# A transformer layer on one core: the modulation stage in another order, and half of the gate-weight rounds moved to a later stage

## The chip, the cores and the metric

The kernel runs on 1 of the 8 cores of a Trainium2 chip. The metric is the device time of one execution in microseconds (us). The engines are named as the profile names them: PE is TensorE (matrix multiplication), DVE is VectorE, ACT is ScalarE, POOL is GpSimd, SP is SyncE, which here issues all the DMAs from one queue. All data are 32-bit; the matrix products are made from a high and a low part of each operand, three products for one, so that they keep the accuracy of 32 bits.

## The reference

One layer of a generator works on 1024 latent tokens (rows of x) and 256 context tokens, each 1024 wide. Cut to what matters here:

```
mod = silu(c) @ w_ada + b_ada          # 6 sections of 1024: shift, scale, gate, shift, scale, gate
mod_c = silu(c_ctx) @ w_ada + b_ada    # the same for the context tokens
px = (rms_norm(x, g_pre_mix) * (1 + scale) + shift) @ w_in      # and pc from ctx, with mod_c
# the columns of px: attention q, k, v; mLSTM q, k, v, output gate, and 16 gate values a token
att = window_attention(...)            # 8 heads, band of 128, all context keys, a sink
h   = mlstm(...)                       # 4 heads, forward and backward, with a state from the context
x   = x + gate * rms_norm(concat(att, h) @ w_out)
x   = x + gate_f * rms_norm(swiglu(modulated norm of x))
```

Only the first part concerns the change: the shift and scale of the first sub-layer, the modulated tokens, their product with w_in, and the gate weights of the mLSTM, which for each chunk of 128 tokens n and each direction d are exp(a + u + mask), a 128 x 128 matrix for each of 4 heads.

## The kernel before

The tokens lie in 10 tiles of 128: tiles 0 to 7 are latent, 8 and 9 are context. Work goes through stages.

*The modulation stage.* Shift and scale come in quarters q = 0 to 3, each 256 columns of both sections. A quarter needs four weight tiles wm (512 KB each). pr_mm(q, h) is half h of its product on TensorE (8 matmuls), mod_row(q) takes the result out of PSUM with ScalarE and VectorE, mod_t(q) turns it into columns (4 transposes), and mod_col(q) adds up and multiplies on VectorE, into hs. In the meantime tiles 0, 1 and 2 (ET = 3) are normalised: prep_c(i) squares on ScalarE, takes the root there and the reciprocal on VectorE, and scales the tile on GpSimd; its two parts can be called apart. prep_t(i) transposes the tile on TensorE, and t_cp(i, b, engine) copies half b out of PSUM. For a quarter q of a tile i, h_ts (VectorE) applies scale and shift, h_hi (ScalarE) makes the high part hh, h_lo (VectorE) the low part hl. w_hi and w_lo do the same for that quarter of the weight columns (w1 is 272 wide, w2 is 384). sq(i, q) then does the 12 matmuls of tile i and quarter q into two PSUM tiles ("slab"); a callback can be put in its middle. warm(n) issues n matmuls of ones that nothing reads. ld("...") gives the order of the loads: x is a token tile, m a wm tile, w a quarter of the weight columns. The order of all this is written out by hand: pin keeps an instruction behind what was traced before it on its engine.

*The slab stage.* Tiles 3 to 9 go through prep_l (load), prep_c, prep_t, prep_m, prep_b and then s1 (24 matmuls with the 272 columns) and s2 (24 with the 384). For tiles 6 to 9 a transposed copy (xtr) is loaded as hraw, and only the root is spread over partitions by a matmul (L235); eight VectorE steps (L256) scale it. gates() works out the gate values in a long chain of small operations, with s2 of tiles 4 to 9 as TensorE's other work.

*Gate weights.* ml_weights(n), for n = 0 to 7, loads two rows of a_d, spread over 128 partitions (256 KB each), does 8 VectorE additions (L640) and 2 exponentials on ScalarE (L641) on them, and stores 512 KB in w_dr[n] (L642). Eight such rounds stand here. The attention stage loads w_dr[n] back (ml_load, L897).

*The transposed stage.* For the 13 tiles of 128 columns in TILES (mk0, mk1, ak, mq0, mq1, aq0 to aq3, mo0 to mo3), tload(j) loads and splits the weights, tproj multiplies, and a convolution, a rotation or a sigmoid follows. From mq0 on, state_step (transposes pk at L803, key scratch at L805, products pu at L809) advances the mLSTM state after each tile, in 9 steps. ada_rest sums up the later modulation sections on VectorE (L751) from loads of 512 KB.

*The attention and mLSTM stage* has 16 items of half a block; the first eight also do one mLSTM block each (ml_scores, ml_values at L1053 and L1057). What follows, the output projection and the feed-forward part, is not touched.

The scratch buffers R0 to R15 are 16 regions of SBUF. R(k, name, shape) gives region k to a new tile. A new tile in a region waits for the last use of the one before it, wherever in the program that use is written. So mkc, the context keys with the scratch kps of all state steps, keeps region 8 until the last state step. Region 8 is also that of the round weights w2 and w7, and of qz of the second mLSTM block.

Outside the pinned instructions a planner orders each engine's work by a timing model of its own.

## Time and profile before

| | us |
|---|---|
| median of 3 runs (lowest, highest) | 1179.77 (1179.26, 1180.34) |
| the profiled execution's own time | 1177.58 |
| its span in the trace | 1175.8 |

| engine | busy us | share of the span |
|---|---|---|
| PE | 1153.5 | 98% |
| DVE | 774.1 | 66% |
| ACT | 551.0 | 47% |
| POOL | 147.5 | 13% |

The span is the time from the first to the last instruction in the trace, 1.8 us less than the execution's own time. Matmuls overlap, so a busy PE is not necessarily at its peak. The mean granted clock of TensorE is 0.997. Rows of the trace begin with the start and the length in us, then engine, source line, operation, output and inputs; "x8" is the number of instructions in the row, and in brackets stands how long the engine had been idle and what ended it.

### The profile page before, as it was taken

What the parts mean: (1) busy time and instruction counts of PE and PEld (TensorE: products, weight loads), DVE (VectorE), ACT (ScalarE), POOL (GpSimd) and SP (SyncE); (2) the same over time, 40 slices, a digit from 0 to 9 for tenths busy, and PEclk for the clock granted to TensorE, in tenths of its full rate; (3) what the DMA queues carried; (4) which work ended last, traced back from release to release, by engine and by line L of the source; (5) the groups of instructions that cost most, each with busy time, mean ns of one, the idle gap of its engine ahead of it and who ended that gap; (6) DMA issues with size and microseconds to landing.
All of it is one profiled execution on the core that took longest, in us unless ns stands there. A gap on an engine that the chain in (4) does not pass through costs nothing.

```text
span 1175.8 us, 16321 instructions
## 1 busy us (share of the span) xinstructions
PE 1153.5 (98%) x5905; PEld 950.8 (81%) x5905; DVE 774.1 (66%) x1417; ACT 551.0 (47%) x1032; POOL 147.5 (13%) x200
## 2 busy tenths in 40 slices
PE   8989989999999999999999999999999999999997
PEld 6789878878888777888788888888888888888886
DVE  4673858882787653469677767777677756644557
ACT  4553444222777864887443333333343434434543
POOL 1240002144655640000000000000000000000000
PEclk9999999999999999999999999999999999999999
DMA  9621954657798605220334566555644458666853
GB/s 372 228 95 50 382 218 133 196 168 220 224 247 217 179 19 179 92 88 36 99 135 159 196 219 223 206 206 213 220 158 140 174 200 271 208 207 193 298 189 125
DMA packets 102984, 216.99 MB, mean 185 GB/s; under 512 B 10228, under 2 KB 39540, under 8 KB 101496
## 3 DMA queue, kind: packets, MB, share of 16 engines
q1 hardware_dynamic: 102904, 215.95, 55.3%
q8 instruction: 46, 0.75, 0.3%
q14 instruction: 34, 0.28, 0.1%
HBM read 159.29 MB, written 55.97 MB: 183 GB/s over the span
## 4 chain that ended last, share of the span: by engine, by line
PE 94%; DVE 3%; ACT 1%; DMA 1%; issue 0%; DVEq 0%; SPq 0%; POOL 0%; ACTq 0%; POOLq 0%
PE xv L79 8%; PE xv L77 8%; PE xv L78 8%; PE pt L79 6%; PE pt L77 6%; PE pt L78 6%; PE t L701 4%; PE t L700 4%; PE t L703 4%; PE pt L1155 3%; PE pt L1137 3%; PE op L79 2%; PE op L78 2%; PE op L77 2%; PE fx L77 2%; PE fx L79 2%
## 5 line engine op out<-in xcount | busy, mean ns | idle before, releaser
L66 DVE TENSOR_TENSOR fo<-fr,fo 128x1024 fp32r<-128x1024 f32 x77 | 93.0, 1223 | 72.4 <-ACT fo L65 69.3
L65 ACT CAST fo<-fr 128x1024 fp32r<-128x1024 f32 x77 | 79.5, 1051 | 74.0 <-PE pt L79 34.8
L700 PE MATMUL t<-hh,th 128*128 128x512 f32 x208 | 82.6, 398 | 0.0
L701 PE MATMUL t<-hl,th 128*128 128x512 f32 x208 | 81.9, 394 | 0.0
L1537 ACT CAST wS<-wr 128x512 fp32r<-128x512 f32 x88 | 54.2, 622 | 55.4 <-PE pt L79 36.8
L1539 DVE TENSOR_TENSOR wS<-wr,wS 128x512 fp32r<-128x512 f32 x88 | 60.4, 689 | 19.8 <-ACT wS L1537 19.7
L703 PE MATMUL t<-hh,tl 128*128 128x512 f32 x208 | 66.6, 394 | 0.0
L79 PE MATMUL xv<-tT,wS 128*128 128x512 f32 x168 | 65.7, 391 | 0.0
L77 PE MATMUL xv<-tT,wS 128*128 128x512 f32 x168 | 65.7, 391 | 0.0
L78 PE MATMUL xv<-tT,wS 128*128 128x512 f32 x168 | 65.6, 390 | 0.0
L77 PE MATMUL op<-woh,mh 128*128 128x512 f32 x128 | 50.9, 398 | 0.0
L79 PE MATMUL op<-woh,ml 128*128 128x512 f32 x128 | 50.1, 392 | 0.6 <-DVE ml L66 0.6
L78 PE MATMUL op<-wol,mh 128*128 128x512 f32 x128 | 50.0, 391 | 0.0
L1285 DVE TENSOR_TENSOR wr<-wr 128x512 f32<-128x512 f32 x66 | 45.5, 690 | 1.4
L700 PEld LDWEIGHTS t<-hh,th 128*128 128x128 f32 x208 | 39.4, 189 | 8.4 <-issue 0.3
L701 PEld LDWEIGHTS t<-hl,th 128*128 128x128 f32 x208 | 39.4, 189 | 7.8 <-issue 0.8
L1571 ACT ACTIVATE es<-es 128x512 f32<-128x512 f32 x22 | 13.9, 632 | 66.5 <-DVE es L1288 66.5
L703 PEld LDWEIGHTS t<-hh,tl 128*128 128x128 f32 x208 | 37.8, 189 | 7.0 <-issue 0.5
L77 PE MATMUL pt<-fo 128*128 128x512 f32 x110 | 42.8, 389 | 0.0
L78 PE MATMUL pt<-fo 128*128 128x512 f32 x110 | 42.8, 389 | 0.0
L79 PE MATMUL pt<-fo 128*128 128x512 f32 x110 | 42.8, 389 | 0.0
L874 PE MATMUL s<-k,qh 128*128 128x256 f32 (+1 forms) x128 | 41.7, 336 | 0.5 <-DVE sm L876 0.5
(792 smaller groups left out, 3303.2 us busy)
## 6 DMA issues: line engine op xcount, KB each, us to landing
wr<-in_wfi SPq DMA_DIRECT2D x44, 512.0 KB, 5.0
wb<-in_wada SPq DMA_DIRECT2D x24, 512.0 KB, 7.6
s_d<-a SPq DMA_DIRECT2D x22, 512.0 KB, 6.4
bt<-in_wfo SPq DMA_DIRECT2D x44, 256.0 KB, 3.7
tb_d<-bt SPq DMA_DIRECT2D x11, 1024.0 KB, 3.8
fr<-s_d SPq DMA_DIRECT2D x44, 256.0 KB, 4.3
fr<-tb_d SPq DMA_DIRECT2D x44, 256.0 KB, 4.3
fr<-a_d SPq DMA_DIRECT2D x33, 256.0 KB, 4.5
```

Of the source, the lines that this page charges most:

```text
L65: act.copy(hi, raw)
L66: dve.tensor_tensor(lo, raw, hi.bitcast(F32), SUB)
L77: pe.matmul(ps, a[0], b[0], start=first, stop=False, **kw)
L78: pe.matmul(ps, a[0], b[1], start=False, stop=False, **kw)
L79: pe.matmul(ps, a[1], b[0], start=False, stop=last, **kw)
L700: pe.matmul(o, wh[:, kt], m[0], start=f, stop=False)
L701: pe.matmul(o, wh[:, kt], m[1], start=False, stop=False)
L703: pe.matmul(o, wl[:, kt], m[0], start=False, stop=l)
L874: pe.matmul(o, qh[:, h, :], k2[g][:, kc], start=True, stop=False)
L1285: dve.tensor_tensor(out, a, b, SUB)
L1537: act.copy(w[:, 0], raw)
L1539: dve.tensor_tensor(w[:, 1], raw, w[:, 0].bitcast(F32), SUB)
```

## The change

- The ten token tiles and their scratch hraw get other regions (the two lists of region numbers in prep_l); x1 and x2 are loaded earlier, and all remaining tile loads are queued before the loop over the slabs.
- The stage's order is rewritten: tile 1 and tile 2 are prepared earlier, the high halves of the weight columns are made one by one, and tile 1's transposes go into the middle of the first sq. In sq the products with the low half of the tokens come last. The fillers warm(1) and warm(3) go, warm(6) becomes warm(8). Two more PSUM tiles use the tag tp. The evictions of tiles 0 to 2 are pinned, and tile 5's normalisation comes behind the first of them.
- ml_weights(0) to (3) stay where they are, in regions 6, 7, 8 and 15. Rounds 4 to 7 are written at the ends of the tiles mo0, mo1 and mo2 of the transposed stage, all in region 8.

```diff
@@ -197,19 +197,19 @@
     def prep_l(i):
 
         j = i - NT
-        xt = xts[i] = R(4 + i % 4, f"xt{i}", (D,))
+        xt = xts[i] = R((4, 5, 6, 7, 4, 5, 10, 6, 13, 15)[i], f"xt{i}", (D,))
         xd[i] = dma(xt, x[i * P:(i + 1) * P] if i < NT else ctx[j * P:(j + 1) * P])
-        hraw[i] = R((0, 1, 2, 3, 10, 11, 12, 13, 8, 9)[i], f"hraw{i}", (KT, P))
+        hraw[i] = R((0, 1, 2, 3, 8, 9, 11, 12, 14, 7)[i], f"hraw{i}", (KT, P))
         return xd[i]
 
     def prep_c(i, parts=(0, 1)):
 
         xt, r = xts[i], st[:, 10 + i:11 + i]
-        if 1 not in parts:
+        if parts == (0,):
             pin(act.activation(hraw[i].rearrange("p a b -> p (a b)"), xt, AF.Square, accum_out=st[:, i:i + 1]))
             pin(act.activation(r, st[:, i:i + 1], AF.Sqrt, bias=epst, scale=1.0 / D))
             return
-        if 0 not in parts:
+        if parts == (1,):
             pin(dve.reciprocal(r, r))
             pin(pool.tensor_scalar(xt, xt, r, 1.0, MUL, MUL))
             return
@@ -299,7 +299,7 @@
 
     def pr_mm(q, h):
         if not h:
-            prs_[q] = pa.tile([P, 512], F32, name=f"pr{q}", tag="gx" if q < 3 else "tp", bufs=2)
+            prs_[q] = pa.tile([P, 512], F32, name=f"pr{q}", tag="gx" if q < 2 else "tp", bufs=2)
         for t in range(4):
             pin(pe.matmul(prs_[q][32 * t:32 * t + 32], cz[:, 4 * h + t, :], was[q, 2 * h + t // 2][:, t % 2],
                           start=not h, stop=h == 1))
@@ -311,7 +311,7 @@
     pcl = {}
 
     def mod_t(q):
-        pcl[q] = pa.tile([P, 4, P], F32, name=f"pcol{q}", tag="gx" if q < 2 else "tp", bufs=2)
+        pcl[q] = pa.tile([P, 4, P], F32, name=f"pcol{q}", tag="gx" if q < 1 else "tp", bufs=2)
         for k in range(4):
             pin(pe.transpose(pcl[q][:, k, :], rr[:, k * P:(k + 1) * P], ident))
 
@@ -332,9 +332,9 @@
         return ((w1h[b][:, k:k + 2], w1l[b][:, k:k + 2], w[:, 0:544].rearrange("p (k n) -> p k n", k=2)),
                 (w2h[b][:, k:k + 2], w2l[b][:, k:k + 2], w[:, 544:1312].rearrange("p (k n) -> p k n", k=2)))
 
-    def w_hi(q):
-        for h_, l_, w in w_(q):
-            pin(act.copy(h_, w))
+    def w_hi(q, i):
+        h_, l_, w = w_(q)[i]
+        pin(act.copy(h_, w))
 
     def w_lo(q, i):
         h_, l_, w = w_(q)[i]
@@ -366,19 +366,21 @@
         b, k0 = q // 2, 2 * (q % 2)
         (a1, l1), (a2, l2) = ((w1h[b], w1l[b]), (w2h[b], w2l[b]))
         A, B = sps[i]
-        n = 0
-        for w, o, lo_, f, e in ((a1, A, 0, 1, 0), (a2, B, 0, 1, 0), (l1, A, 0, 0, 0), (a1, A, 1, 0, 1), (a2, B, 1, 0, 0), (l2, B, 0, 0, 1)):
+        x_ = [(a1, A, 0), (a2, B, 0), (l1, A, 0), (l2, B, 0), (a1, A, 1), (a2, B, 1)]
+        if not i + q:
+            x_ = [x_[j] for j in (0, 2, 4, 1, 5, 3)]
+        for n, (w, o, lo_) in enumerate(x_):
+            if mid and n == 3:
+                mid()
             for k in (k0, k0 + 1):
                 h_ = (hl if lo_ else hh)[b][:, k, i * P:(i + 1) * P]
-                r = pin(pe.matmul(o, h_, w[:, k], start=bool(f) and not q and k == k0, stop=bool(e) and q == 3 and k > k0))
-                n += 1
-                if mid and n == 6:
-                    mid()
+                f, e = o not in [z[1] for z in x_[:n]], o not in [z[1] for z in x_[n + 1:]]
+                r = pin(pe.matmul(o, h_, w[:, k], start=f and not q and k == k0, stop=e and q == 3 and k > k0))
         return r.ins
 
     dve.tensor_copy(bb[:, 0], bcol(0))
     dve.tensor_scalar(bb[:, 1], bcol(1), 1.0, None, ADD)
-    ld("x0 m00 m01 m02 m03 w0 x1 m10 m11 m12 m13 w1 x2")
+    ld("x0 m00 m01 m02 m03 x1 w0 x2 m10 m11 m12 m13 w1")
     warm(20)
     prep_c(0)
     pr_mm(0, 0)
@@ -391,89 +393,94 @@
     mod_row(0)
     warm(2)
     mod_t(0)
-    w_hi(0)
+    prep_c(1, (0,))
     mod_col(0)
-    warm(6)
+    prep_c(1, (1,))
+    warm(8)
     h_ts(0, 0)
+    w_hi(0, 0)
     h_hi(0, 0)
+    w_hi(0, 1)
     w_lo(0, 0)
     h_lo(0, 0)
     w_lo(0, 1)
     ld("w2")
-    sq(0, 0)
-    prep_c(1)
+    sq(0, 0, lambda: prep_t(1, True))
+    prep_c(2, (0,))
+    t_cp(1, 0, dve)
+    h_ts(1, 0)
+    t_cp(1, 1, act)
+    h_hi(1, 0)
+    prep_c(2, (1,))
+    h_lo(1, 0)
     pr_mm(1, 0)
-    warm(1)
-    prep_t(1, True)
-    t_cp(1, 0, act)
-    h_ts(1, 0)
-    h_hi(1, 0)
-    t_cp(1, 1, dve)
-    h_lo(1, 0)
-    warm(3)
+    sq(1, 0)
     pr_mm(1, 1)
-    ld("m30 m31 x3 m32")
+    ld("m30 m31 m32 m33 x3")
+    prep_t(2, True)
     mod_row(1)
-    sq(1, 0, lambda: mod_t(1))
-    w_hi(1)
+    t_cp(2, 0, act)
+    h_ts(2, 0)
+    mod_t(1)
+    w_hi(1, 0)
+    h_hi(2, 0)
+    w_hi(1, 1)
     mod_col(1)
+    h_lo(2, 0)
+    sq(2, 0)
     h_ts(0, 1)
     h_hi(0, 1)
+    t_cp(2, 1, act)
     w_lo(1, 0)
+    w_lo(1, 1)
     h_lo(0, 1)
-    w_lo(1, 1)
-    ld("w3 m33 x4")
+    ld("w3 x4")
     sq(0, 1)
-    prep_c(2)
     h_ts(1, 1)
     h_hi(1, 1)
     h_lo(1, 1)
     pr_mm(2, 0)
-    sq(1, 1)
-    prep_t(2, True)
-    t_cp(2, 0, act)
-    h_ts(2, 0)
-    h_hi(2, 0)
+    h_ts(2, 1)
+    h_hi(2, 1)
+    h_lo(2, 1)
     pr_mm(2, 1)
     mod_row(2)
-    h_ts(2, 1)
-    h_hi(2, 1)
-    t_cp(2, 1, act)
-    h_lo(2, 0)
-    h_lo(2, 1)
-    sq(2, 0, lambda: mod_t(2))
-    w_hi(2)
+    sq(1, 1, lambda: mod_t(2))
+    w_hi(2, 0)
+    w_hi(2, 1)
+    w_lo(2, 0)
     mod_col(2)
     h_ts(0, 2)
     h_hi(0, 2)
-    w_lo(2, 0)
+    w_lo(2, 1)
     h_lo(0, 2)
-    w_lo(2, 1)
     sq(2, 1)
-    h_ts(1, 2)
-    h_hi(1, 2)
-    h_lo(1, 2)
+    sq(0, 2)
+    for i in (1, 2):
+        h_ts(i, 2)
+        h_hi(i, 2)
+        h_lo(i, 2)
     pr_mm(3, 0)
-    sq(0, 2)
-    h_ts(2, 2)
-    h_hi(2, 2)
-    h_lo(2, 2)
+    pr_mm(3, 1)
     prep_c(3, (0,))
-    w_hi(3)
+    mod_row(3)
     prep_c(3, (1,))
+    sq(1, 2, lambda: mod_t(3))
+    w_hi(3, 0)
+    w_hi(3, 1)
+    mod_col(3)
+    h_ts(0, 3)
+    h_hi(0, 3)
     w_lo(3, 0)
+    h_lo(0, 3)
     w_lo(3, 1)
     pool.memset(V[:, :, :, 128:129], 1.0)
     pool.memset(Vc[:, :, :, 128:129], 1.0)
-    sq(1, 2)
-    pr_mm(3, 1)
-    mod_row(3)
     prep_c(4, (0,))
-    sq(2, 2, lambda: mod_t(3))
-    mod_col(3)
     prep_c(4, (1,))
+    sq(2, 2)
     prep_t(3, True)
-    for i in range(ET):
+    for i in (1, 2):
         h_ts(i, 3)
         h_hi(i, 3)
         h_lo(i, 3)
@@ -500,15 +507,15 @@
     def s1(i):
         s1_out(i, slab(i, 272, w1h, w1l))
 
-    def s1_out(i, ps):
+    def s1_out(i, ps, pin=lambda z: z):
         sf = i + 2 if i < NT else i - NT
         sb = 9 - i if i < NT else 1 - (i - NT)
         dve.tensor_tensor(G[:, 0:2, sf, :], ps[:, 0:8].rearrange("p (k h) -> p k h", h=4),
                           bcr[:, 0:8].rearrange("p (k h) -> p k h", h=4), ADD)
         dve.tensor_tensor(G[:, 2:4, sb, :], ps[:, 8:16].rearrange("p (k h) -> p k h", h=4),
                           bcr[:, 8:16].rearrange("p (k h) -> p k h", h=4), ADD)
-        act.copy(av[:, i], ps[:, 16:144].rearrange("p (g v) -> p g v", v=64))
-        act.copy(vrow(i)[:, 0, 0:128], ps[:, 144:272])
+        pin(act.copy(av[:, i], ps[:, 16:144].rearrange("p (g v) -> p g v", v=64)))
+        pin(act.copy(vrow(i)[:, 0, 0:128], ps[:, 144:272]))
 
     NI = NT + NC_
     NFILL = 3
@@ -525,23 +532,24 @@
             act.copy(vrow(i)[:, 1:4, 0:128], s2ps.pop(i)[:, 0:384].rearrange("p (h v) -> p h v", v=128))
 
     chain(lambda: dma(bcr, bcast(bcv)))
+    chain(prep_l, 5)
+    chain(lambda: dma(cst, const))
+    for i in range(XT, NI):
+        chain(prep_l, i)
+        chain(lambda: dma(hraw[i], xtr[i - XT]))
     for i in range(ET):
         sqe = sq(i, 3)
-        s1_out(i, sps[i][0])
-        act.copy(vrow(i)[:, 1:4, 0:128], sps[i][1].rearrange("p (h v) -> p h v", v=128))
+        s1_out(i, sps[i][0], pin)
+        pin(act.copy(vrow(i)[:, 1:4, 0:128], sps[i][1].rearrange("p (h v) -> p h v", v=128)))
         if not i:
             prep_b(3)
+            prep_c(5)
         if i == 1:
             prep_t(4, True)
-    chain(prep_l, 5)
-    chain(lambda: dma(cst, const))
-    prep_c(5)
     ch += [R(i, f"ch{i}", (4, L), F32R) for i in range(2)]
     cl += [R(2 + i, f"cl{i}", (4, L), F32R) for i in range(2)]
     for i in range(ET, NI):
         if i + 3 < NI:
-            chain(prep_l, i + 3)
-            chain(lambda: dma(hraw[i + 3], xtr[i + 3 - XT]))
             prep_c(i + 3)
         if i + 1 < NI:
             prep_b(i + 1)
@@ -631,7 +639,7 @@
 
     def ml_weights(n):
 
-        wt_ = R((6, 7, 8, 15, 5)[n % 5], f"w{n}", (2, 4, P))
+        wt_ = R((6, 7, 8, 15)[n] if n < 4 else 8, f"w{n}", (2, 4, P))
         for d in range(2):
             s_, r0 = rows_of(n, d)
             w = wt_[:, d]
@@ -657,10 +665,8 @@
             s2(i)
         if i in (NFILL + 1, NFILL + 2):
             tload(i - NFILL - 1)
-        if i > NFILL:
+        if NFILL < i < NFILL + 5:
             ml_weights(i - NFILL - 1)
-    for n in range(NI - NFILL - 1, NT):
-        ml_weights(n)
     close(p1)
 
 
@@ -1002,6 +1008,8 @@
                 cst_[k] = R(k, f"cs{k}", (2, 2, 2, 129))
             for d in range(2):
                 state_step(d, s_)
+        for n in {"mo0": (4, 5), "mo1": (6,), "mo2": (7,)}.get(name, ()):
+            ml_weights(n)
     close(htp)
     close(psA)
```

## Prediction

> **What bounds the kernel now.** I read the page's totals first, then the busy time of the engines by stretches, then the list of waits.
>
> ```profile
> span 1175.8 us, 16321 instructions
> PE 1153.5 (98%) x5905; PEld 950.8 (81%) x5905; DVE 774.1 (66%) x1417; ACT 551.0 (47%) x1032; POOL 147.5 (13%) x200
> ```
>
> TensorE is busy nearly all the time, so the change can win only where TensorE idles or runs slowly: some 22 us of the span. The stretches show where this lies near the edited code; a row gives start and end, length, busy us and instructions of PE, PEld, DVE, ACT and POOL, the granted clock, the DMA share and GB/s.
>
> ```profile
> 16.00:56.50 40.50, 36.38 (x245) 28.26 (x246) 27.97 (x77) 18.95 (x45) 7.86 (x8) 1.00 0.74 281
> 20.00:25.00 5.00, 4.47 (x34) 3.19 (x32) 3.25 (x12) 2.61 (x5) 0.00 (x0) 1.00 1.03 410
> 71.00:80.00 9.00, 5.39 (x29) 4.98 (x28) 8.87 (x24) 4.74 (x10) 5.90 (x9) 0.81 0.09 10
> 170.00:178.00 8.00, 3.90 (x18) 2.81 (x18) 6.04 (x11) 3.97 (x8) 0.68 (x1) 0.79 0.21 69
> 288.00:340.00 52.00, 51.65 (x387) 43.91 (x385) 38.84 (x135) 38.26 (x108) 30.73 (x43) 1.00 0.81 228
> ```
>
> The first row is the modulation stage: 4.1 us idle. The second, inside it, shows the transfers at full rate. The third and fourth each hold a hole, and a lower granted clock after it: 3.6 us idle plus 9 x 0.19 = 1.7 us lost to the clock, and 4.1 + 8 x 0.21 = 5.8 us. The last row is the place to which half of the gate-weight rounds will move; TensorE has no hole there. The waits that end those holes:
>
> ```profile
> PE slab L373 <- ACT hh L355: 3.4, 6, 1.2
> PE slab L77 <- ACT hh L273: 3.6, 2, 2.6
> PE pk L803 <- ACT cr L714: 1.9, 1, 1.9
> ```
>
> All are waits for a ScalarE output at the end of a chain of small steps, not for bandwidth.
>
> **Part 1: the modulation stage (new order, own buffers, high halves first).** No arithmetic is removed. Of the filler matmuls, warm(1) and warm(3) go (8 records; six take 0.83 with the last one's tail, a step of 0.125 us, so 1.0 us of TensorE time), and two are added before the first slab, in a wait. Rows for the steps:
>
> ```profile
> 14.85 0.60 DVE L352 TENSOR_SCALAR hraw<-hraw,hs 128x128 f32<-128x128 f32 x2
> 15.86 1.06 ACT L216 ACTIVATE hraw<-xt 128x1024 f32<-128x1024 f32 x1
> 16.01 0.52 PE L373 MATMUL slab<-w1h,hh 128*128 128x272 f32 x2 [0.85 <-ACT hh L355]
> 17.04 0.29 ACT L219 ACTIVATE st<-st,epst 128x1 f32<-128x1 f32 x1
> 18.02 1.07 PE L304 MATMUL pr<-wm,cz 128*32 128x512 f32 x8
> 19.34 1.04 PE L241 MATMUL pt<-vec,xt 128*128 128x128 f32 x8
> 20.21 0.83 PE L280 MATMUL warm<-ones 128*128 128x128 f32 x6
> 22.93 0.60 PE L316 MATMUL pcol<-vec,av 128*128 128x128 f32 x4
> 27.11 1.39 DVE L352 TENSOR_SCALAR hraw<-hraw,hs 128x128 f32<-128x128 f32 x2
> 27.28 1.14 POOL L224 TENSOR_SCALAR xt<-xt,st 128x1024 f32<-128x1024 f32 x1 [8.54 <-DVE st L220]
> 40.96 0.41 PE L373 MATMUL slab<-w1h,hh 128*128 128x272 f32 x2
> 42.41 0.51 PE L373 MATMUL slab<-w2l,hh 128*128 128x384 f32 x2
> 56.13 0.51 PE L373 MATMUL slab<-w2l,hh 128*128 128x384 f32 x2
> ```
>
> One quarter of one token tile (sq) takes TensorE 1.8 us (40.96 to 42.41, and 0.35 for the last pair: six matmuls of 272 columns in steps of 0.125 and six of 384 in steps of 0.175). One half of a modulation product (pr_mm) takes 1.0, a token tile's 8 transposes 0.9, mod_t 0.5 (their rows less the last matmul's tail). I laid the new program order out by hand with these.
>
> - Until mod_col(0) ends, just ahead of the row at 14.85, nothing differs. Now tile 1's square and root (1.5 us of ScalarE, as from 15.86 to the end of the root at 17.33) run right after mod_row, so tile 1's scaling on GpSimd falls at about 15.05, onto h_ts(0,0). The two rows at 27.11 show what that costs: the pair of tensor_scalars takes 1.39 us instead of 0.60. So the first slab starts at about 16.85, 0.85 later than now.
> - Then it pays: tile 1's transposes run inside sq(0,0), which ends at 19.6. pr(1,0) goes to 20.6, and sq(1,0) follows at once, where now its transposes, copies, a cast and two groups of fillers stand between.
> - Going on: sq(1,0) ends 22.4, pr(1,1) 23.4, tile 2's transposes 24.3, mod_t(1) 24.9, a wait of 0.9 for tile 2's high half (in it the 0.3 that mod_t(1) now waits for a PSUM buffer of tag tp, till tile 2's first copy is out), sq(2,0) 27.6, sq(0,1) 30.0, both halves of pr(2) 32.0, sq(1,1) with mod_t(2) 34.35, sq(2,1) and sq(0,2) 37.95, pr(3) 39.95. There mod_row(3) stands behind tile 3's square on ScalarE, so mod_t(3) waits 0.9; sq(1,2) ends 43.2, sq(2,2) 45.0, tile 3's transposes 45.9, sq(0,3) 47.7, and sq(2,3) 52.5 after tile 4's transposes.
>
> Now the stage ends at 56.5 (the row at 56.13 and its 0.35). So the term is -4.0 us. Its bounds: the 4.1 idle and 1.0 of fillers, -5.1, and nothing. Loads are no limit: modulation product 1 needs its data at 19.6, and moving x1 and x2 forward delays that by one 512 KB load, 1.3 us at the 410 GB/s of this stretch, while now it runs at 18.02.
>
> **Part 2: token tiles 5 to 9 (own buffers).**
>
> ```profile
> 57.05 1.07 ACT L216 ACTIVATE hraw<-xt 128x1024 f32<-128x1024 f32 x1
> 64.76 0.33 SPq L201 DMA_DIRECT2D xt<-in_ctx  x1
> 67.54 0.61 PE L235 MATMUL pt<-vec,st 128*128 128x128 f32 x4
> 69.02 3.96 DVE L256 SCALAR_TENSOR_TENSOR hraw<-hraw,hs,pt 128x128 f32<-128x128 f32 x15
> 74.85 0.97 DVE L274 TENSOR_TENSOR hl<-hraw,hh 128x512 fp32r<-128x512 f32 x1
> 75.59 0.59 PE L77 MATMUL slab<-w1h,hh 128*128 128x272 f32 x1 [2.60 <-ACT hh L273]
> ```
>
> The last tile's load is issued only at 64.76, because its buffer was tile 5's. Tile 5's square starts at 57.05, after the slab stage. VectorE has gaps until then and next is overrun: 15 steps of 0.26 us for tiles 6 and 7 stand ahead of tile 6's low half at 74.85, and TensorE waits. With the new regions no load of tiles 5 to 9 waits for a transpose later than tile 3's (45.9 in the order above), and tile 5's square moves behind the first eviction (about 48 instead of 57). Then tile 5's transposes fit at about 52, tile 6's 8 steps (2.1 us) at 54 to 56, GpSimd's two additions and the cast by 60, while TensorE needs tile 6 only after s1(3), s2(3), s1(4), s1(5): 52.5 + 3.0 + 4.2 + 3.0 + 3.0 (24 steps of 0.125 for an s1, of 0.175 for an s2) and transposes, about 66.5. So the hole goes: -3.6 and its clock loss -1.7, together -5.3. Bounds: -5.3 and 0, since the planner may order VectorE badly again.
>
> On the clock, the Trainium skill ("TensorE: Matmul & The Clock Gate", Part 1) says that about 3.4 us of idling halves the clock until a busy window of the same length has passed. By it a remaining hole of 2 us could cost its length alone, and a partial success would save 1.7 us more than in proportion. No term of my sum uses that.
>
> **Part 3: gate-weight rounds 4 to 7 leave the stretch from 117 to 157.**
>
> ```profile
> w<-a_d SPq DMA_DIRECT2D x16, 256.0 KB, 6.9
> w_dr<-w SPq DMA_DIRECT2D x8, 512.0 KB, 9.4
> L640 DVE SCALAR_TENSOR_TENSOR w<-w,ucol,mF 128x128 f32<-128x128 f32 x32 | 9.2, 351 | 0.6 <-DMA w<-a_d 0.6
> L641 ACT ACTIVATE w<-w 128x512 f32<-128x512 f32 x16 | 10.1, 633 | 17.4 <-DVE w L640 17.4
> 155.79 0.33 SPq L642 DMA_DIRECT2D w_dr<-w  x1
> 162.86 1.28 ACT L722 ACT_TABLE_LOAD   x1 [3.21 <-DMA w_dr<-w]
> ```
>
> The row at 162.86 is the cause of the hole at 170: mkc shares buffer 8 with round 7, whose store is issued at 155.79, so the convolution's output waits for it. The second key tile's convolution comes behind, and the state steps (pk, L803) behind that. With rounds 4 to 7 gone, buffer 8 is free after round 2's store, some 20 us earlier, and the chain needs about 8 us, so it is done by 160, ten before TensorE asks. Term: -5.8. Bounds: -5.8 and 0.
>
> The rounds come back later. Buffer 8 then belongs to mkc until its last use, and mkc holds the key scratch of every state step. So rounds 4 to 7 can't start where they are written, but only after the last state step, and one after the other.
>
> ```profile
> 287.60 1.10 PE L809 MATMUL pu<-V,mkc 128*64 128x129 f32 x16
> 300.88 1.41 DVE L1044 TENSOR_TENSOR wl<-wl,s 128x256 f32<-128x256 f32 x4
> 305.09 1.06 ACT L1199 ACTIVATE so<-so 128x1024 f32<-128x1024 f32 x1
> 310.37 0.61 PE L1053 MATMUL pt<-cs,qz 128*128 128x129 f32 x4
> wl<-w_dr SPq DMA_DIRECT2D x6, 512.0 KB, 4.9
> ```
>
> The last state step ends at 288.7. Each round brings VectorE 8 steps of 0.285 us (in pace), 2.3 us, and ScalarE 2 x 0.63: for four, 9.2 and 5.1 us, in a stretch where they are busy 38.84 and 38.26 of 52. The bounds are 0 (13 us of VectorE are free) and +9.2 (all of it in line). The chain of waits runs over VectorE and ScalarE from 300.9 to 308.4 (first and last parts shown at 300.88 and 305.09), 7.5 of the first 20 us, so I take that share: 9.2 x 7.5 / 20 = +3.4. Four rounds also move 4 MB to a stretch with a DMA share of 0.81, and their stores stand on SP's queue ahead of query loads; I count nothing for it, as the queue waits now too and TensorE doesn't, and keep it for the range.
>
> **The sum:** -4.0 - 5.3 - 5.8 + 3.4 = -11.7 us. The profiled execution took 1177.58 us; 1165.9 is its counterpart. The median of the runs is 2.2 us above it, so I forecast 1168.1 for the median. What follows at 340 and later is TensorE-bound and only shifts.
>
> **Rivals.**
> *Buffer 8 becomes the bound (slower).* Buffer 8 next goes to qz of the second mLSTM block. A round takes at least 4.9 (a load, as wl's row) + 1.2 + 1.2 (the two directions' steps) + 0.7 + 4.9 (the store) = 12.9 us, with today's 6.9 and 9.4 up to 19.4. Four end at 340 to 366, and the block that now runs at 310.4 gets its operand 30 us late or more. If TensorE, which takes its work in order, stands for it, the time is 1179.8 - 15.1 + 30 = 1195. It decides once TensorE waits over 15 us there. For it: the shared buffer. Against: eight of the sixteen attention items follow without an mLSTM block, so the planner has other matmuls to put in front. 0.15.
> *One hole stays.* If VectorE's order at 70, or ScalarE's at 170, is as bad as now, 5.5 us of the sum go: 1173.6. For it: both holes come from an order that a planner chose. 0.20.
> *The moved rounds are free and the first stage gives all:* -5.1 - 5.3 - 5.8 = -16.2, 1163.6. 0.10.
> *The first stage gives nothing and the hole at 70 stays:* -5.8 + 3.4, 1177.4, hardly to be told from no change. For it: the four scalings of tiles 1 to 4 on GpSimd now each meet VectorE work, and 4 x 0.8 us (1.39 against 0.60) eats 3.2 of the 4.0. The Trainium skill ("SBUF — State Buffer", Who interferes with whom) says that the later of the two "fully blocks" until the other ends. By it each meeting would cost up to the 1.1 us of the scaling, 4.5 in all; the row at 27.11 agrees with it in kind. 0.10.
>
> **How the numbers follow.** The likeliest case has 0.45 and its own range is 1163 to 1173. From 1160 to 1178 lies about 0.8: that case, the free one, one hole left, and half of the last. 0.2% of 1179.77 is 2.4 us, about what a measurement can tell. Faster: 0.45 + 0.20 + 0.10 = 0.75; same 0.10; slower 0.15.
>
> **What would show it.** Right: the last L373 matmul near 52 us; tile 6's slab without a wait and a clock of 1.00 through the slab stage; no wait before the first pk; L640 steps after the last pu. Wrong: TensorE waits for hh (L273), for L1053's qz, or for L876 behind L640 between 280 and 350; a table load more per moved round.

## The result and the profile after

The changed kernel takes 1199.52 us (median, 1198.59 to 1200.55) against 1180.05 of the kernel before in the same batch: a ratio of 1.0165, 95% interval 1.0148 to 1.0183. It is slower by 19.5 us, where 1168.1 and a gain were forecast. The profiled execution has a span of 1197.8 us, 22.0 more than before.

The page's first lines show hardly more work: the busy times grew by 2.4 us (VectorE) to 4.6 us (ScalarE), the span by 22.

```profile
span 1197.8 us, 16313 instructions
...
PE 1156.4 (97%) x5901; PEld 952.3 (80%) x5901; DVE 776.5 (65%) x1417; ACT 555.6 (46%) x1035; POOL 152.0 (13%) x200
```

So nearly the same work waits longer. To find where, I take the first and last start of some lines in both traces; behind the count of a row stand its durations (ns: least, median, most), then the first and last start. Before, with the first projection (L700), the state updates' transposes and products (L803, L809) and the out-projection (L77):

```profile
L700 PE MATMUL t<-hh,th x208: 387/390/776, 117.2 to 296.9; 128*128 128x512 f32 x104
...
L803 PEld LDWEIGHTS pk<-vec,mk x28: 138/139/223, 203.0 to 282.5; 128*128 128x128 f32 x28
...
L809 PEld LDWEIGHTS pu<-V,mkc x112: 132/137/138, 208.8 to 288.3; 128*64 128x64 f32 x112
...
L77 PEld LDWEIGHTS op<-woh,mh x128: 187/188/191, 432.7 to 536.5; 128*128 128x128 f32 x128
```

After, the same places have line numbers 6 higher (L706, L809, L815):

```profile
L706 PE MATMUL t<-hh,th x208: 387/389/497, 112.4 to 285.3; 128*128 128x512 f32 x104
...
L809 PEld LDWEIGHTS pk<-vec,mk x28: 138/140/224, 191.9 to 270.9; 128*128 128x128 f32 x28
...
L815 PEld LDWEIGHTS pu<-V,mkc x112: 132/136/137, 198.0 to 276.7; 128*64 128x64 f32 x112
...
L77 PEld LDWEIGHTS op<-woh,mh x128: 186/188/190, 454.0 to 558.4; 128*128 128x128 f32 x128
```

The first projection starts 4.8 us earlier (117.2 to 112.4), the first of these state updates 11.1 (203.0 to 191.9), the last state product 11.6 (288.3 to 276.7). The out-projection starts 21.3 us later (432.7 to 454.0). All the loss, 32.9 us, falls between the last state product and the out-projection. By stretches (start and end, length, busy us and instructions of PE, PEld, DVE, ACT and POOL, granted clock, DMA share, GB/s):

```profile
56.50:71.00 14.50, 13.51 (x102) 13.07 (x101) 11.53 (x37) 8.66 (x20) 7.01 (x9) 1.00 0.13 36
71.00:80.00 9.00, 6.73 (x47) 5.87 (x47) 9.00 (x24) 3.22 (x9) 5.51 (x4) 1.00 0.21 60
170.00:180.00 10.00, 10.00 (x67) 8.30 (x66) 6.79 (x9) 2.85 (x3) 2.13 (x4) 1.00 0.14 53
280.00:290.00 10.00, 6.33 (x36) 5.22 (x34) 1.58 (x6) 1.90 (x6) 0.31 (x2) 0.94 0.73 227
290.00:300.00 10.00, 6.72 (x36) 6.23 (x36) 6.15 (x23) 6.37 (x17) 6.31 (x5) 0.55 0.75 187
300.00:310.00 10.00, 7.00 (x57) 6.26 (x56) 7.86 (x30) 9.94 (x18) 5.24 (x8) 1.00 0.67 212
310.00:320.00 10.00, 6.34 (x39) 4.87 (x38) 9.12 (x29) 7.61 (x20) 2.74 (x4) 0.98 0.96 276
320.00:330.00 10.00, 1.88 (x7) 1.32 (x5) 4.76 (x13) 6.13 (x11) 3.61 (x5) 0.50 0.62 181
330.00:340.00 10.00, 7.28 (x35) 5.18 (x36) 3.09 (x10) 2.47 (x7) 1.31 (x5) 0.67 0.14 39
```

The hole at 170 is gone. At 71 the clock is now 1.00, but TensorE is still idle 2.3 us there and 1.0 us in the row ahead of it, and VectorE is busy for all of the row at 71. From 280 to 340 (the last six rows) TensorE is busy 35.55 of 60 us, where before it was 51.65 of 52, and the granted clock falls to 0.50. In the waits of this stretch (us in total, times, longest):

```profile
DVE w L648 <- DMA w<-a_d: 12.9, 2, 9.1
...
PE pt L1061 <- DMA qz<-q_dr: 8.9, 1, 8.9
...
PE s L880 <- DVE sm L882: 7.0, 4, 5.0
```

and in the trace around the first and the last long one:

```profile
288.42 1.14 DVE L648 SCALAR_TENSOR_TENSOR w<-w,ucol,mF 128x128 f32<-128x128 f32 x4 [9.08 <-DMA w<-a_d]
...
290.53 0.75 DVE L882 CUSTOM_DVE_ANT_0 pr__2690<-s,mask,bcr 128x512 f32<-128x512 f32 x1
...
291.34 0.58 PE L880 MATMUL s<-k,qh 128*128 128x256 f32 x1 [5.01 <-DVE sm L882]
```
```profile
280.40 1.45 SPq L646 DMA_DIRECT2D w<-a_d  x2
...
327.70 0.33 SPq L650 DMA_DIRECT2D w_dr<-w  x1
330.32 11.09 SPq L915 DMA_DIRECT2D qz<-q_dr  x7
```
```profile
332.72 1.20 PE L1061 MATMUL pt<-cs,qz 128*128 128x129 f32 x4 [8.92 <-DMA qz<-q_dr]
```

The moved round 4 is loaded from 280.4. Its sums (L648) stand on VectorE's queue among the first score reads (L882, by which VectorE takes attention scores out of PSUM), two reads ahead of them and six behind. VectorE waits 9.1 us for the load, and the read at 290.53, on which TensorE's next score product hangs, waits with it: TensorE stands 5.0 us. At the other end round 7's store is issued at 327.7, the operand qz of mLSTM block 1 follows in the same buffer at 330.3, and TensorE, which waits for it 8.9 us, goes on at 332.7.

### The profile page after: what moved, and what is told of

It is laid out like the page before. It is cut to its first block, busy times and chain, and to the rows that moved or that the text cites. A ratio compares the mean times of both kernels' runs of the same rounds, so it can differ in the third digit from the quotient of the medians.

```text
span 1197.8 us, 16313 instructions
## 1 busy us (share of the span) xinstructions
PE 1156.4 (97%) x5901; PEld 952.3 (80%) x5901; DVE 776.5 (65%) x1417; ACT 555.6 (46%) x1035; POOL 152.0 (13%) x200
## 4 chain that ended last, share of the span: by engine, by line
PE 82%; DVE 7%; DMA 4%; ACT 2%; SPq 2%; POOL 1%; issue 1%; DVEq 0%; ACTq 0%; POOLq 0%
PE xv L79 8%; PE xv L78 8%; PE xv L77 8%; PE pt L78 6%; PE pt L79 6%; PE pt L77 6%; PE pt L1163 2%; PE pt L1145 2%; PE op L79 2%; PE op L78 2%; PE op L77 2%; PE fx L77 2%; PE fx L79 2%; PE fx L78 2%; PE slab L378 2%; PE t L707 2%
## 5 line engine op out<-in xcount | busy, mean ns | idle before, releaser
L706 PE MATMUL t<-hh,th 128*128 128x512 f32 x208 | 82.3, 396 | 0.0
L77 PE MATMUL xv<-tT,wS 128*128 128x512 f32 x168 | 65.6, 390 | 0.0
L77 PE MATMUL op<-woh,mh 128*128 128x512 f32 x128 | 50.9, 398 | 0.0
L706 PEld LDWEIGHTS t<-hh,th 128*128 128x128 f32 x208 | 39.1, 188 | 8.3 <-issue 0.3
L77 PE MATMUL pt<-fo 128*128 128x512 f32 x110 | 42.8, 389 | 0.0
```

The lines of the kernel that those rows point to most:

```text
L77: pe.matmul(ps, a[0], b[0], start=first, stop=False, **kw)
L706: pe.matmul(o, wh[:, kt], m[0], start=f, stop=False)
```

## The experiments

All medians are in the table; each is compared with the kernel before as run beside it (its median was 1180.05 beside the changed kernel and 1179.1 to 1179.7 in the four batches of experiments).

| run | what differs | median us | ratio to before, 95% interval |
|---|---|---|---|
| changed kernel | | 1199.5 | 1.0148 to 1.0183 |
| rounds_all_early | parts 1 and 2 alone | 1174.4 | 0.9939 to 0.9969 |
| moved_rounds_alone | part 3 alone | 1204.1 | 1.0194 to 1.0225 |
| before_not_in_8 | before, round 7 in buffer 6 instead of 8 | 1171.6 | 0.9918 to 0.9948 |
| early_not_in_8 | parts 1 and 2, rounds early, round 7 in 6 | 1167.6 | 0.9881 to 0.9911 |
| one_round_moved | early_not_in_8, round 7 moved | 1173.6 | 0.9942 to 0.9972 |
| one_round_behind_block0 | the same, its sums later | 1172.4 | 0.9925 to 0.9959 |
| two_rounds_moved | rounds 6 and 7 moved | 1185.6 | 1.0046 to 1.0073 |
| sums_behind_scores | four moved, sums later | 1199.8 | 1.0157 to 1.0202 |
| qz1_in_15 | four moved, qz of block 1 in 15 | 1189.8 | 1.0067 to 1.0101 |
| sums_behind_and_qz1_in_15 | both | 1189.5 | 1.0065 to 1.0115 |
| rounds_in_15 | four moved, in 15, sums later | 1188.7 | 1.0069 to 1.0097 |
| four_rounds_spread | four moved, in 15, sums spread | 1182.1 | 1.0015 to 1.0035 |
| moved_without_sums | four moved, without arithmetic | 1192.5 | 1.0088 to 1.0135 |
| early_subtract_on_gpsimd | early_not_in_8, subtraction moved | 1167.4 | 0.9885 to 0.9927 |
| early_squares_sooner | the same, squares sooner | 1170.3 | 0.9913 to 0.9938 |

**Which part loses.** Parts 1 and 2 alone: the changed kernel with the old place and buffers of the rounds.

```diff
-        wt_ = R((6, 7, 8, 15)[n] if n < 4 else 8, f"w{n}", (2, 4, P))
+        wt_ = R((6, 7, 8, 15, 5)[n % 5], f"w{n}", (2, 4, P))
...
-        if NFILL < i < NFILL + 5:
+        if i > NFILL:
             ml_weights(i - NFILL - 1)
+    for n in range(NI - NFILL - 1, NT):
+        ml_weights(n)
...
-        for n in {"mo0": (4, 5), "mo1": (6,), "mo2": (7,)}.get(name, ()):
-            ml_weights(n)
```

> The changed kernel with all eight gate-weight rounds back at their old place and in their old buffers, so parts 1 and 2 of the change alone. The marks of the two traces say: up to the first transposed projection the change gains 5.0 us (117.2 to 112.2), up to the last state update 11.6 (288.3 to 276.7), and 32.9 are lost after that (last out-projection start 433.3 to 454.6). Theory (the moved rounds alone make the loss, by whatever way): the hole of 6 us at 170 is back, the stretch from 277 to 340 is free of holes, time 1180 - 5 = 1174 to 1176. Rival (the loss comes from the new order of parts 1 and 2, or from a different order that the planner finds with everything earlier): about 1199, with TensorE idle for some 24 us between 280 and 340 as now.

1174.4: the gain of parts 1 and 2 is 5.0 us, and nothing is lost at 280 (TensorE is busy 59.6 of the 60 us from 280 to 340). Part 3 alone, on the kernel before, is the opposite edit:

> The kernel before with part 3 alone: rounds 4 to 7 moved behind the state steps of the later stage, in buffer 8. Theory (the parts add up): 1180 - 6 (no hole at 170) + 33 (the loss after the last state update) = 1205 to 1208. Rival (the loss needs the earlier start that parts 1 and 2 give, or hangs on how the planner happens to order things): under 1195.

1204.1, a little under the range expected. It is 24.7 us above the kernel before (1179.4), and the changed kernel is 25.1 above rounds_all_early (1199.5 - 1174.4), so the parts add up and the moved rounds alone make the loss.

**Buffer 8 and the hole at 170.** The rounds go back to their old place, by the lines shown above, and only round 2 uses buffer 8. In before_not_in_8 the same numbers stand in the kernel before, which changes nothing else; of the old numbers only that of round 7 differs, 6 for 8:

```diff
-        wt_ = R((6, 7, 8, 15)[n] if n < 4 else 8, f"w{n}", (2, 4, P))
+        wt_ = R((6, 7, 8, 15, 5, 6, 7, 6)[n], f"w{n}", (2, 4, P))
```

> The changed kernel with all eight rounds at their old place, but rounds 4 to 7 in buffers 5, 6, 7 and 6 instead of one of them in 8: only round 2 uses buffer 8. Theory (the hole at 170 comes from buffer 8 alone, the loss at 280 from the moved rounds alone): no hole at 170 and none at 280, time 1180 - 11.6 = 1168 to 1170. Rival (the hole at 170 is from VectorE's and ScalarE's work on eight rounds, not from the buffer): hole of 4 us or more at 170 with buffer 8 free, 1174 to 1176.

> The kernel before with one edit: gate-weight rounds 5 to 7 use buffers 6, 7 and 6 instead of 6, 7 and 8, so the convolution's output in buffer 8 waits for round 2 only. Nothing moves. Theory (the hole at 170 is that buffer's): no hole at 170, 5 to 7 us less than before, 1172 to 1175. Rival (VectorE's and ScalarE's work for the rounds holds the convolution too): 1177 to 1180.

1167.6 and 1171.6. The stretch of the hole in rounds_all_early, early_not_in_8 and before_not_in_8:

```profile
160.00:180.00 20.00, 15.54 (x69) 11.64 (x68) 11.99 (x18) 8.81 (x17) 2.64 (x5) 0.83 0.23 61
```
```profile
160.00:180.00 20.00, 20.00 (x112) 16.67 (x111) 13.13 (x17) 11.95 (x18) 3.15 (x6) 1.00 0.29 86
```
```profile
160.00:180.00 20.00, 19.65 (x100) 15.78 (x99) 12.76 (x24) 12.19 (x19) 2.67 (x5) 1.00 0.43 132
```

With eight early rounds, and no more than one line of new buffer numbers, the hole is gone (20.00 and 19.65 busy against 15.54, clock 1.00 against 0.83). It was the buffer and not the rounds' work. The edit is worth 6.8 us on parts 1 and 2 (1174.4 to 1167.6) and 8.1 on the kernel before, more than the 5.8 that I gave the hole. early_not_in_8 is faster than both kernels: it has all the gains of the change without the move.

**Why the moved rounds lose: the buffer or VectorE's order.** First block 1's operand alone leaves buffer 8:

```diff
-                qz[n] = R((13, 8)[n], f"qz{n}", (2, 2, 2, P))
+                qz[n] = R((13, 15)[n], f"qz{n}", (2, 2, 2, P))
```

> The changed kernel with the query operand qz of mLSTM block 1 in buffer 15 instead of 8; nothing else changes, so the four moved rounds still follow one another in buffer 8, and their sums stand in the same order on VectorE. Theory buffer 8 (my rival of the prediction: block 1 waits for the last moved round's store, all else follows): all 33 us go, about 1167 to 1170. Theory VectorE's queue (the sums of a round wait at the head of VectorE's queue for their load, 9.1 us for the first one, and the score reads behind them keep TensorE waiting): only the last hole goes, 8.9 us and about 3 us of lower clock, 1186 to 1190. Theory load (the rounds' work and their 4 MB are too much for the stretch): 1195 to 1200.

1189.8, the value of the queue theory; the hole for qz is gone, but TensorE's first hole has grown from 5.0 to 8.7 us. Here buffer 15 is held by the third gate's store, which took 8.1 us to land, and round 4's load stands behind block 1's operand. Then the order alone: the sums go behind the eight first score reads.

```diff
-        for n in {"mo0": (4, 5), "mo1": (6,), "mo2": (7,)}.get(name, ()):
-            ml_weights(n)
+        if name == "mo3":
+            for n in (4, 5, 6, 7):
+                ml_weights(n)
...
+                if n > 3:
+                    pin(r_)
...
+            if early:
+                pin(r_)
```

(`pin` keeps program order: the first is a sum, the second one of the eight score reads.)

> The changed kernel with one order written out by hand: VectorE's sums of the moved rounds come behind its eight first score reads, where now the sums of round 4 stand among them (two reads, round 4, six reads). Buffers and work are as in the change. Theory VectorE's queue alone: the hole of 5.0 us at 286 and the lower clock after it (0.55 from 290 to 300) go and stay gone, 1190 to 1192. Theory two limits in a row (with buffer 8 as in the change, the four rounds still follow one another from 280 to 330, and block 1's operand comes no earlier): the time saved at 286 is waited for at block 1, whose hole grows from 8.9 to some 15 us or more, 1195 to 1200. Theory load: 1195 to 1200 too, but with TensorE's idle time spread and no hole of over 10 us.

> The order of the run sums_behind_scores and the buffer of the run qz1_in_15 together, all four rounds moved. Theory two limits in a row (VectorE's queue and buffer 8 are all there is): nearly all of the loss goes, 1168 to 1173, with no hole of over 2 us between 280 and 340. Theory load (four rounds' sums, exponentials and 4 MB cost time there by themselves): 1178 or more, with TensorE idle 8 us or more in that stretch.

1199.8 and 1189.5. In sums_behind_scores the hole at 286 is gone (TensorE busy 10.00 from 280 to 290), but nothing is gained by that: the time is waited for later, most of it in two holes.

```profile
320.32 0.66 PE L882 MATMUL s<-k,qh 128*128 128x384 f32 x1 [6.36 <-DVE sm L897]
...
333.33 1.20 PE L1066 MATMUL pt<-cs,qz 128*128 128x129 f32 x4 [11.61 <-DMA qz<-q_dr]
```

So two limits stand in a row, as expected: buffer 8 sets when block 1 can go on (333.3 here, 332.7 in the changed kernel), whatever is gained ahead of it. But with both removed 1189.5 is far from the 1168 to 1173 that this theory gave, so it is not the whole. TensorE there waits 3.2 us (to 298.9) and 3.7 us (to 338.5) for products of gate weights that stand behind the sums of a moved round on VectorE; ahead of each of them four sums took 3.9 and 4.0 us, where four take 1.1 elsewhere. The same with the rounds in 15 and qz in 8:

```diff
-        wt_ = R((6, 7, 8, 15)[n] if n < 4 else 8, f"w{n}", (2, 4, P))
+        wt_ = R((6, 7, 8, 15)[n] if n < 4 else 15, f"w{n}", (2, 4, P))
```

> All four rounds moved, their sums behind the first score reads, but in buffer 15 instead of 8: block 1's operand qz follows the last state update in buffer 8 as in the kernel before, and the moved rounds follow the third gate's store, which buffer 15 holds until about 287. The first moved load then stands at the head of the transfer queue until that store has landed, some 7 us, with block 1's operand and the loads of the third and fourth attention item behind it. Theory chain (only the coupling of block 1 to the rounds costs): 1168 to 1172. Theory transfer queue (what stands behind the first moved load comes late by those 7 us): 1175 to 1188, with TensorE waiting for operands between 288 and 310. Theory load: 1190 or more.

1188.7, between the ranges of the last two theories. TensorE waits 3.1 us for a product of gate weights and 4.1 and 3.9 us at score products, each time for VectorE and at most 0.7 us for anything else.

**Chain or arithmetic.**

```diff
-            for h in range(4):
+            for h in range(4 if n < 4 else 0):
...
-            act.activation(w, w, AF.Exp)
+            if n < 4:
+                act.activation(w, w, AF.Exp)
```

> The changed kernel with the sums and exponentials of rounds 4 to 7 left out (those four operands are then wrong); their loads and stores stay, one after the other in buffer 8. Theory two limits in a row: no VectorE wait for a load, so no hole at 286; the chain of four loads and stores is some 2 to 3 us a round shorter and ends near 318 instead of 330, so a hole of some 5 to 10 us stays at block 1: 1180 to 1190. Theory load by arithmetic (VectorE and ScalarE are overrun): all of the loss goes, 1167 to 1171. Theory load by transfers: 1195 or more.

1192.5, a little above the chain's range. No wait at 286, but the chain of loads and stores in buffer 8 alone holds block 1 for 15.1 us, longer than expected:

```profile
322.18 1.20 PE L1062 MATMUL pt<-cs,qz 128*128 128x129 f32 x4 [15.11 <-DMA qz<-q_dr]
```

Without any arithmetic of the four rounds 24.9 us of the loss over early_not_in_8 remain (1192.5 - 1167.6). TensorE's only other wait of over 2 us is 2.4 us for an operand of attention. So the loads and stores in one buffer, with block 1 behind them, cost time without any sum. How much of it is the shared buffer, and how much the transfers themselves, is not shown: no run has them without sums and with block 1 in another buffer.

**Fewer rounds.** Rounds 0 to 6, or 0 to 5, stay early and only round 2 of them in 8; the rest is moved, in buffer 8, with the sums behind the score reads as above. For one round:

```diff
-        wt_ = R((6, 7, 8, 15)[n] if n < 4 else 8, f"w{n}", (2, 4, P))
+        wt_ = R((6, 7, 8, 15, 5, 6, 7, 6)[n] if n < 7 else 8, f"w{n}", (2, 4, P))
...
+        if name == "mo3":
+            for n in range(7, NT):
+                ml_weights(n)
```

> Rounds 0 to 6 at the old place (rounds 4 to 6 in buffers 5, 6, 7; only round 2 in 8), round 7 alone moved, in buffer 8, its sums behind the first score reads as in sums_behind_scores. In that run the first moved round's store was issued at 296.6 and the second's at 307.4, the operand of block 1 landed 2.2 to 2.6 us after the last store, and in early_not_in_8 block 1 begins at 307.3. Theory chain (rounds in line in buffer 8, block 1 behind them): one round ends before block 1 needs the buffer, no loss: 1167 to 1170. Theory load (the loss of some 32 us is shared evenly by the four rounds): 1175 to 1177.

> As one_round_moved, with rounds 6 and 7 moved. Theory chain: block 1's operand at about 310, 3 to 6 us after it is needed, and the lower clock after that hole: 1171 to 1178. Theory load: half of the loss, 1183 to 1186.

1173.6 and 1185.6: 6.0 and 18.0 us over early_not_in_8; four in the same order (sums_behind_scores) cost 32.2. With two rounds block 1 waits 3.6 us for qz, as the chain theory had it, but TensorE also waits 3.1, 1.2 and 1.1 us for what stands behind the sums, and the time is above the chain's range. One round should have been free by the chain theory and was not. In one_round_moved:

```profile
291.15 2.79 POOL L902 TENSOR_SCALAR pr__2713<-pr__2713,sm 128x512 f32<-128x512 f32 x4
...
291.28 2.80 DVE L648 SCALAR_TENSOR_TENSOR w<-w,ucol,mF 128x128 f32<-128x128 f32 x4
...
294.01 1.13 DVE L648 SCALAR_TENSOR_TENSOR w<-w,ucol,mB 128x128 f32<-128x128 f32 x4
...
295.05 1.41 DVE L1059 TENSOR_TENSOR wl<-wl,s 128x256 f32<-128x256 f32 x4
...
295.52 0.71 PE L1072 MATMUL pt<-V,wl 128*128 128x129 f32 x4 [3.12 <-DVE wl L1059]
```
```profile
290.00:300.00 10.00, 5.89 (x31) 5.04 (x30) 9.08 (x24) 6.61 (x13) 6.05 (x10) 0.83 0.67 186
```

The eight sums take 3.9 us on VectorE (2.80 + 1.13), not the 2.3 that I counted; the slow four run beside GpSimd's scaling of the softmax rows. Behind them stands the product of block 0's gate weights (L1059, in this kernel's numbers), for which TensorE waits 3.1 us; after the hole the clock is low, 0.83 in the mean. 4.1 us idle and 10 x 0.17 of clock are 5.8, near the 6.0 measured.

**Place or amount.** What was then open: does a round cost this much because of what stands behind its sums? The sums go behind the product of block 0's gate weights; and all four rounds in buffer 15, each behind the product of one of the blocks 0 to 3. (In both, `pin` now keeps the order of these products and no longer that of the score reads.)

```diff
     ml_scores(0)
+    ml_weights(7)
```

For four_rounds_spread that is `ml_weights(4)`, and in the loop over the items:

```diff
                 ml_scores(i + 1)
+                if i < 3:
+                    ml_weights(i + 5)
```

> As one_round_moved, but the sums of round 7 come behind the product of block 0's gate weights with its scores on VectorE, where there they stood just ahead of it (TensorE waited 3.1 us for that product, and the granted clock was 0.83 from 290 to 300). Theory place (the sums cost only by what stands behind them on VectorE): 1167 to 1170, no wait of over 1 us from 285 to 310. Theory amount (a moved round costs 6 us wherever its sums stand): 1172 to 1175.

> All four rounds moved, in buffer 15 as in rounds_in_15, but the sums of rounds 4, 5, 6 and 7 each behind the product of block 0, 1, 2 and 3, so spread over some 80 us instead of following one another. Theory place: the waits for block products and score reads (3.1, 4.1 and 3.9 us in rounds_in_15) go, 1168 to 1174; what may stay is a wait for the operands behind the first moved load on the transfer queue. Theory amount: about as rounds_in_15, 1185 to 1190.

1172.4 and 1182.1: the first as by amount, the second between the two. In one_round_behind_block0 the wait for the product is gone and the one for the next score read has come (first fence); the second fence shows the clock behind it, and the third one round's sums in four_rounds_spread, the GpSimd instruction beside them and the hole behind them.

```profile
296.72 0.48 PE L884 MATMUL s<-k,qh 128*128 128x384 f32 x1 [2.35 <-DVE sm L886]
```
```profile
297.00:298.00 1.00, 1.00 (x6) 1.00 (x6) 1.00 (x4) 1.00 (x2) 0.43 (x1) 0.50 0.65 258
...
299.00:300.00 1.00, 1.00 (x7) 1.00 (x6) 0.90 (x5) 1.00 (x3) 0.65 (x3) 0.50 0.00 0
300.00:301.00 1.00, 1.00 (x9) 1.00 (x9) 0.00 (x0) 0.56 (x2) 0.47 (x2) 0.80 0.22 66
```
```profile
320.29 3.44 DVE L648 SCALAR_TENSOR_TENSOR w<-w,ucol,mF 128x128 f32<-128x128 f32 x4 [1.39 <-DMA w<-a_d]
...
320.67 2.39 POOL L1125 TENSOR_TENSOR woxl<-wor,woxh 128x1024 fp32r<-128x1024 f32 x1
...
325.64 0.69 PE L882 MATMUL s<-k,qh 128*128 128x384 f32 x1 [5.12 <-DVE sm L884]
```

In each of the places tried, something that TensorE needs next stands behind the sums. VectorE is not full in this stretch (38.84 of 52 us before), but its order has little slack. Spread, four rounds cost 14.5 us (1182.1 - 1167.6), 3.6 each. In line in buffer 8 they cost 32.

**What is left at 56 to 80.** Two edits of early_not_in_8 at token tiles 6 to 9: one of two subtractions on GpSimd, then also the squares, roots and reciprocals one step sooner.

```diff
-            dve.tensor_tensor(ls[b][:, :, tok], raws_[b], h_.bitcast(F32), SUB)
+            (pool if i >= XT and b else dve).tensor_tensor(ls[b][:, :, tok], raws_[b], h_.bitcast(F32), SUB)
```

> The run early_not_in_8 with one edit at token tiles 6 to 9: the subtraction for the second half's low part (one of two per tile, 0.67 to 1.45 us on VectorE) goes to GpSimd. In early_not_in_8 TensorE is idle 3.2 us from 56.5 to 80 and VectorE is busy 9.00 of the 9 us from 71 to 80. Theory (VectorE's load is what is left of part 2's hole): 1 to 2.5 us less than early_not_in_8, 1165 to 1167. Rival (GpSimd and VectorE slow each other, and GpSimd's additions for the next tile now come later): same or up to 4 us more, 1168 to 1172.

```diff
-        if i + 3 < NI:
+        if i == ET:
             prep_c(i + 3)
+        if i + 4 < NI:
+            prep_c(i + 4)
```

> The run early_subtract_on_gpsimd, and the squares, roots and reciprocals of token tiles 7 to 9 one step of the loop earlier (TensorE waits twice 0.9 us for a reciprocal there, which stands behind 8 or 16 sums of 0.26 us on VectorE). Theory (VectorE's order is what is left at 56 to 80): 1 to 2 us less, 1165 to 1167. Rival (the 24 sums of tiles 6 to 8 now stand together ahead of tile 6's subtraction): a hole of 2 us or more at tile 6's low part, 1168 to 1172.

1167.4 and 1170.3. The same stretch in early_not_in_8, early_subtract_on_gpsimd and early_squares_sooner:

```profile
71.00:80.00 9.00, 6.75 (x48) 5.91 (x48) 9.00 (x24) 3.19 (x9) 5.51 (x4) 1.00 0.20 60
```
```profile
71.00:80.00 9.00, 7.63 (x57) 7.00 (x56) 6.84 (x17) 4.34 (x11) 8.30 (x6) 1.00 0.27 76
```
```profile
71.00:80.00 9.00, 8.51 (x52) 7.84 (x51) 7.23 (x18) 2.70 (x8) 8.11 (x7) 0.81 0.17 52
```

The first edit takes VectorE from 9.00 to 6.84 and gives TensorE back 0.9 us there, and the first projection starts 1.5 us earlier than in early_not_in_8 (110.7 for 112.2). The time doesn't show it: between 160 and 250 TensorE has three waits for VectorE, of 1.5, 1.0 and 0.6 us, that early_not_in_8 doesn't have. Why the order there is another I did not settle. The second edit gives TensorE 0.9 us more in the row and loses it to a clock of 0.81, behind waits of 0.8 and 0.7 us between 68 and 70. Its first projection starts at 112.8, so 2.1 of the some 3 us by which it is worse than the first stand there already.

## Why the prediction was wrong

**Part 1, right in the total, with some luck in the steps.** Forecast -4.0, the end of the first slabs "near 52" for 56.5. The last slab matmuls of this stage and the next group's start:

```profile
52.15 0.52 PE L378 MATMUL slab<-w2h,hl 128*128 128x384 f32 x2
52.51 0.28 PE L77 MATMUL slab<-w1h,hh 128*128 128x272 f32 x1
```

52.5 for 56.5, -4.0. Several steps of the layout held: the first slab starts later than before (16.2 for 16.0; 16.85 was forecast), tile 1's scaling meets h_ts (1.41 us for the pair, 1.39 forecast), and its transposes run inside sq(0,0). But small errors cancel. mod_col(0) already ends 0.5 us earlier than before, ahead of all edited steps. The layout's own prices give 51.6 and not 52.5: sq(0,1) (27.6 to 30.0) and the last steps (47.7 to 52.5) stand in it 0.6 and 0.3 us longer than what they are made of. The wait of 0.9 at mod_t(3) did not come, so that sq(1,2) ended at 41.9 for 43.2, and later one of 1.3 came that the layout does not have:

```profile
47.90 0.52 PE L378 MATMUL slab<-w1h,hh 128*128 128x272 f32 x2 [1.31 <-ACT hh L355]
```

The high half there waits for h_ts, whose pair takes 1.62 us instead of 0.60, from 45.8, beside GpSimd's additions for tile 3 (45.3 to 47.3). So the meetings of VectorE and GpSimd, on which a rival built, did happen, but they did not eat the term.

**Part 2, wrong in size.** Forecast -5.3. From the end of the first slabs to the first projection it took 117.2 - 56.5 = 60.7 and now 112.4 - 52.5 = 59.9: -0.8. The loads were early (the last tile's is issued at 40.2, before at 64.8) and the clock stays at 1.00, as expected, but TensorE is still idle 3.3 us from 56.5 to 80 (13.51 busy of 14.50 and 6.73 of 9.00). I took the late loads for the cause and laid out tile 6's eight steps at 54 to 56. They ran from 64, together with tile 7's, behind the matmul that spreads the root (L235), which starts at 63.6 and ahead of which TensorE was not idle:

```profile
64.04 4.22 DVE L256 SCALAR_TENSOR_TENSOR hraw<-hraw,hs,pt 128x128 f32<-128x128 f32 x16 [0.94 <-PE pt L235]
```

So VectorE had idle time up to there and was overrun behind it (9.00 of 9.00 us busy), much as before; an order chosen by the planner was the reason that the prediction gave for its other bound, 0. That VectorE's load counts there, early_subtract_on_gpsimd shows in part, by its first projection 1.5 us earlier. About 1 us of the difference I cannot place: 3.6 us idle and 1.7 of clock before against 3.3 idle after would be -2.0. It lies in TensorE's busy time, which less the clock's 1.7 was 55.4 us before and is 56.6 now.

**Part 3a, right in mechanism, and somewhat undersized.** Forecast -5.8. From the first projection to the first of the state updates 85.8 us have become 79.5, -6.3; the two pairs of runs give -6.8 and -8.1.

**Part 3b, the step that failed.** Forecast +3.4 with +9.2 as upper bound; measured +32.9. Three things were wrong in it.
- The bound itself. I priced the rounds by VectorE's own time, "all of it in line", and nothing above it. But an engine that stands in order at the head of its queue costs by what it waits for: 9.1 us for one load. And the sums were longer than their row of 117 to 157, where GpSimd was busy 1.35 of 52.8 us (117.2 to 170): rounds 4 and 5 took 2.3 us each, but rounds 6 and 7 took 3.2 to 3.4.
- "I count nothing for it, as the queue waits now too and TensorE doesn't": the chain of loads and stores in buffer 8 that I priced for the rival at 12.9 us a round I left out of the sum. It ran from 280.4 to 330.3, 12.5 a round, and in moved_without_sums the loads and stores alone, with what stands behind them, cost 24.9 us.
- The weight of the rival. "Buffer 8 becomes the bound" had the place, nearly the pace of the chain, and 1195; it got 0.15 on the argument that the planner has other matmuls to put in front of block 1. It put them there (TensorE's wait for qz is 8.9 us and not 30), but there were waits among them too, so that the time came out above the rival's. The rival's condition, over 15 us of waiting in one place, was wrong for the same reason: the loss was spread over several waits.

Of the other signs of being wrong, the score product behind the rounds' sums came as named (5.0 us), the wait for hh (L273) is down from 3.6 to 0.3 us, and the table loads on ScalarE rose from 13 to 16, which says little, as early_not_in_8 has 15 without a moved round.

The rival was not the whole story either: with block 1's operand out of buffer 8 (qz1_in_15) only 9.7 of 32 us came back. TensorE then waits 8.7 us for a score read behind round 4's sums, and with the sums behind the reads as well it waits for products of gate weights behind the later sums (3.2 and 3.7 us). A moved round cost 3.6 to 6 us even where TensorE doesn't wait for qz. How these 3.6 to 6 divide between the sums' own time, GpSimd and the clock in each place I did not separate, nor the share of the transfer queue in rounds_in_15.

**GpSimd, the right rule at the wrong place.** The row at 291.28 shows sums in steps of 0.70 us beside GpSimd work that starts together with them, and the row at 294.01 steps of 0.28 without. The Trainium skill ("SBUF — State Buffer", Who interferes with whom) says that a VectorE instruction with two SBUF inputs contends with a GpSimd instruction that reads SBUF. The trace agrees. The prediction drew on that section for tile scalings in part 1 only, and not for the sums that it moved into a stretch in which GpSimd is busy 30.73 of 52 us.

## What to carry to other kernels

Work moved to a place where engines have free time is priced by what it waits for and by what stands behind it on each in-order queue, not by its own duration against the free share; four serial rounds in one buffer, each a load, a sum and a store, were a chain of 50 us in front of the buffer's next user. If a rival's arithmetic gives +15 and the argument against it is that the scheduler will find something else to do, it deserves more than 0.15. And when a shared buffer makes a wait, try the buffer's number first: that edit alone gave 8 us here, and the move lost 32.
